# Sixty-four bytes of padding behind each buffer of the split weights

## Chip, cores and metric

The kernel runs on one core of a Trainium2 chip, in one launch. The metric is device time in microseconds of one execution, the median over repeated runs. Times in the text are microseconds (us) unless marked ns.

## What is computed

One layer of a hybrid streaming-encoder block on 256 tokens of width 2,048, in float32:

```python
h = rms_norm(x, mix_norm)
proj = h @ w_in                          # 2048 x 10320, cut into the inputs of both branches
# branch A: causal conv + SiLU, L2-normed q and k, chunked gated delta rule, gated RMSNorm -> o_a
# branch B: latent attention (compressed KV, shared rotary key, block-causal mask)         -> o_b
y = sigmoid(gate_a) * (o_a @ w_branch_a) + sigmoid(gate_b) * (o_b @ w_branch_b)
x = x + y @ w_out
x = x + square(relu(rms_norm(x, mlp_norm) @ w_mlp_up)) @ w_mlp_down      # 2048 -> 8192 -> 2048
x = x + sigmoid(rms_norm(x, ple_norm) @ w_ple_gate) * (p @ w_ple)
```

## The kernel before

**Split operands.** TensorE multiplies in the rounded float32 type `F32R`. To keep float32 accuracy each operand X is written as hi + lo: ScalarE (ACT) copies X into an F32R tile (`act.copy(hi, src)`), and VectorE (DVE) subtracts (`lo = src - hi`). Of the four products the kernel adds three: hi·hi, hi·lo and lo·hi.

**The weight stream.** All large products run in one long loop, `stream`. The weights lie in HBM in the order of use. A step is two 128-row slices of one group of at most 512 columns. `load(i)` brings the step's 512 KB into one of five `raw` tiles through SP's queue; `cut(i)`, three steps ahead of its use, splits it into one of four `whi` and one of four `wlo` tiles; then come the step's matmuls.

**Two kinds of group.** In an ordinary group the activations stand in the array (LDWEIGHTS of 128x128) and the weights move through it, 512 columns at a time; each slice gives six matmuls, all on line L432: for each of two token blocks, activation-hi with `whi`, activation-hi with `wlo`, activation-lo with `whi`. In a turned group (the MLP's up product) the weights stand and the activations `nT` move: per slice four matmuls of 512 columns with `whi` (L425; hi and lo of the 256 tokens side by side) and four of 256 columns with `wlo` (L428). The tiles that hold split activations are `hT`, `cT`, `obT`, `oaT`, `yT`, `nT`, `uT`, `gT` and `pT`; each is 4,096 bytes per partition. The MLP goes up(0), up(1), down(0), up(2), down(1), up(3), down(2), down(3), where up(c) writes `uT` chunk c and down(c) reads it.

**Side work** (norms, transposes, attention, the delta rule) is woven between the steps. Its matmuls are plain float32; the profile records each of them, apart from the transposes, as two passes.

**Pools and places.** Tiles come from pools that lie one behind another in each partition. Behind the weights' pool comes `lpool`, with 23 slots of 4,096 bytes for activations; behind that `tiny`, and then a pool for the mixer's side work whose room the MLP later uses for the pool of the odd `uT` chunks (chunks 0 and 2 are in `lpool`). In `tiny` a 704-byte tile `gap` (`PAD` = 176 floats) is never read. The byte offsets in a partition, as the two built kernels place the tiles:

| tiles | before | after |
|---|---|---|
| `raw`, five | 26,176 + 4,096·n | 26,688 + 4,096·n |
| `whi`, four | 46,656; 50,752; 54,848; 58,944 | 47,168; 51,328; 55,488; 59,648 |
| `wlo`, four | 63,040; 67,136; 71,232; 75,328 | 63,808; 67,968; 72,128; 76,288 |
| `lpool` | 79,424 + 4,096·n | 80,448 + 4,096·n |
| odd `uT` chunks | 187,968 + 4,096·n | 188,992 + 4,096·n |

Before, all but the last row leave 1,600 when divided by 4,096, and the last row leaves 3,648, which is 2,048 more. So the start of every weight tile and the start of every activation tile differ by a multiple of 2,048 bytes; slices of them that meet in one matmul differ by multiples of 512. One pair in the attention is different: `krT` lies at 24,576 (a multiple of 512), `qrT` at 64 bytes past a multiple of 512.

At the start, POOL (GpSimd) clears a tile `spin`, and TensorE runs 14 matmuls on it (L216, output `idle`) while the first weights arrive.

The lines that the prediction speaks of in `stream`:

```python
for j in range(2):
    if g.turned:
        for c in range(4): pe.matmul(ps[c], hi[:, j, cs], g.acts.both(k), ...)           # L425
        for c in range(4): pe.matmul(ps[c][:, :T], lo[:, j, cs], g.acts.both(k)[:, :T])  # L428
    else:
        for tb in range(NT):
            for n_, (part, w) in enumerate(((0, hi), (0, lo), (1, hi))):
                pe.matmul(ps[tb], g.acts.at(k, part, tb), w[:, j, : g.n], ...)           # L432
```

The first operand of `pe.matmul` behind the output stands in the array, the second moves.

Of the kernel before, what the change touches and what calls it, by code (L numbers as in the profile page):

```python
# [9 lines left out]
F32 = mybir.dt.float32  # L10
F32R = mybir.dt.float32r
# [6 lines left out]
P = 128  # L18
# [23 lines left out]
NPIECE = 5  # L42
NSPIN = 14
PAD = 176


def _round12(v):
# [104 lines left out]
def hybrid_block(ctx: ExitStack, tc: tile.TileContext, a, dbg=None):  # L152
    nc = tc.nc
# [6 lines left out]
    wpool = ctx.enter_context(tc.tile_pool(name="wpool", bufs=1))  # L160
# [6 lines left out]
    RAW_BUFS, SPLIT_BUFS, AHEAD, BIG_BUFS = 5, 4, 3, 23  # L167
# [7 lines left out]
    def acc(name):  # L175
        return psA.tile([P, 512], F32, tag="mm", name=name)

    def small(n, name, dt=F32):
        return tiny.tile([P, n], dt, tag=f"t{name}", name=name, bufs=1 if n == 64 else 2)

    gap = tiny.tile([P, PAD], F32, tag="gap", name="gap", bufs=1)
    nc.gpsimd.memset(gap[:, 0:1], 0.0)

# [15 lines left out]
    def load_xT(j):  # L199
        if x_quad[j // 2] is None:  # L200
            x_quad[j // 2] = big(f"xT{j // 2}", shape=(P, 4, T))
        x_pair[j] = x_quad[j // 2][:, 2 * (j % 2) : 2 * (j % 2) + 2, :]
        nc.sync.dma_start(x_pair[j], a["xT"][:, 2 * j : 2 * j + 2, :])
# [24 lines left out]
    def load_rest():  # L228
        tc.keep_in_program_order(nc.sync.dma_start(par, a["par"]))
        yield  # L230
        tc.keep_in_program_order(nc.sync.dma_start(cst, a["cst"]))
        yield
# [29 lines left out]
    def split(hi, lo, src):  # L262

        act.copy(hi, src)
        dve.tensor_tensor(lo, src, hi.bitcast(F32), ALU.subtract)
# [68 lines left out]
    def weave(force=False):  # L334
        clock[0] += 1
        for i in range(len(lanes)):
            n = (clock[1] + i) % len(lanes)
            if (force or clock[0] - lanes[n].last >= lanes[n].gap) and lanes[n].step():
                lanes[n].last = clock[0]
                clock[1] = n + 1  # L340
                return True
        return False

    def until(cond):
        while not cond():
            if not weave(True):
                raise RuntimeError("side work cannot go on")
# [9 lines left out]
    def stream(groups):  # L357
        steps = [(g, k) for g in groups for k in range(0, g.nk, 2)]
        raws, parts = {}, {}

        base, offs = 0, []
        for g, k in steps:
            offs.append(base)
            base += 2 * P * g.n
            PLAN.append((g.srcs, k))

        def load(i):
            n = steps[i][0].n
            t = wpool.tile([P, 2, 512], F32, tag="raw", name=f"raw{i}", bufs=RAW_BUFS)
            src = a["weights"][offs[i] : offs[i] + 2 * P * n].rearrange("(p k n) -> p k n", p=P, k=2)  # L370
            if i == 0:
                for k in range(2):
                    nc.sync.dma_start(t[:, k, :n], src[:, k, :])
            else:
                nc.sync.dma_start(t[:, :, :n], src)
            raws[i] = t

        def cut(i):
            n = steps[i][0].n
            t = raws.pop(i)[:, :, :n]  # L380
            hi = wpool.tile([P, 2, 512], F32R, tag="whi", name=f"whi{i}", bufs=SPLIT_BUFS)
            lo = wpool.tile([P, 2, 512], F32R, tag="wlo", name=f"wlo{i}", bufs=SPLIT_BUFS)
            if i == 0:
                for k in range(2):
                    split(hi[:, k, :n], lo[:, k, :n], t[:, k, :])
            else:
                split(hi[:, :, :n], lo[:, :, :n], t)
            parts[i] = (hi, lo)

        n = len(steps)  # L390
        for i in range(min(RAW_BUFS, n)):
            load(i)
            if i < 3:
                load_xT(i + 1)
        for j in range(4, 8):
            load_xT(j)
        L_CONV.add(load_rest())
        for i in range(min(AHEAD, n)):
            L_TURN.step()
            cut(i)  # L400
        ps, late = None, None
        for i, (g, k0) in enumerate(steps):
            if late and "rx" in done:
                late()
                late = None
            if i + AHEAD < n:
                cut(i + AHEAD)
            if i + RAW_BUFS < n:
                load(i + RAW_BUFS)
            if k0 == 0:  # L410
                if g.before:
                    g.before()
                if g.turned:
                    ps = [g.turned(f"ps{i}_{c}") for c in range(4)]
                else:
                    ps = [acc(f"ps{i}_{tb}")[:, : g.n] for tb in range(NT)]
            hi, lo = parts.pop(i)
            for j in range(2):
                k = k0 + j
                until(lambda: k in g.acts.ready)  # L420
                first, last = k == 0, k == g.nk - 1
                if g.turned:
                    for c in range(4):
                        cs = slice(c * P, (c + 1) * P)
                        pe.matmul(ps[c], hi[:, j, cs], g.acts.both(k), start=first, stop=False)  # L425
                    for c in range(4):
                        cs = slice(c * P, (c + 1) * P)
                        pe.matmul(ps[c][:, :T], lo[:, j, cs], g.acts.both(k)[:, :T], start=False, stop=last)  # L428
# [3 lines that stand above are left out]
                            pe.matmul(  # L432
                                ps[tb], g.acts.at(k, part, tb), w[:, j, : g.n],
                                start=(first and n_ == 0), stop=(last and n_ == 2),
                            )
            if k0 + 2 >= g.nk:
                if "rx" in done:
                    g.evac(ps)
                else:
                    assert late is None  # L440
                    late = bind(g.evac, ps)
            weave()
            weave()
# [864 lines left out]
```

## Time and profile before

| | |
|---|---|
| median of three runs | 1557.18 us (1556.12 to 1558.06) |
| the profiled execution, its own time | 1555.51 us |
| its span, first to last instruction | 1553.6 us |
| TensorE matmuls (PE) busy | 1542.7 us, 99% of the span |
| LDWEIGHTS (PEld) busy | 1309.2 us, 84% |
| DVE, ACT, POOL busy | 979.6, 773.5, 22.8 us |
| granted TensorE clock | 1.000 |

Rows of the profile name source line, engine, operation, output<-inputs and shape. Matmuls are pipelined: a row's "mean ns of one" (some 390 ns for 512 columns) is the time from its start to its modelled end, and overlaps with the next. The pace is the distance from one start to the next, here called the pitch. It is read from the chain that ended last, where a piece "start, length, what xN" is a run of N back-to-back matmuls: the length divided by N is the pitch.

### The profile page before, as it was taken

Reading aid. Unit: us, or ns where it says so; the run is one execution under the profiler, and the core shown is the slowest. Engines: PE = TensorE matmul, PEld = TensorE weight load, DVE = VectorE, ACT = ScalarE, POOL = GpSimd, SP = SyncE. Lnnn points to the kernel's source line nnn. Section 1 sums busy time; section 2 is a strip of 40 time slices with the busy share of each in tenths; the row PEclk is TensorE's granted clock in tenths of the full one; section 3 lists DMA queues with packets and bytes.
Section 4 is the critical chain, followed back from the end, with each engine's and each line's share of the span. In section 5 each row is a group of like instructions: output and inputs, shape, how many; then the busy total and the mean of one; then the engine's idle time right before and its main releaser. Section 6 shows DMA issues by size and latency. Waiting matters only on the chain.

```text
span 1553.6 us, 20822 instructions
## 1 busy us (share of the span) xinstructions
PE 1542.7 (99%) x7760; PEld 1309.2 (84%) x7760; DVE 979.6 (63%) x1715; ACT 773.5 (50%) x1182; POOL 22.8 (1%) x48
## 2 busy tenths in 40 slices
PE   9999999999999999999999999999999999999998
PEld 7998888788888888888888888888888888888888
DVE  6987777965785645755665665556654665555554
ACT  6765776545434544454444443344433443345543
POOL 0000001000100000000000000000000000000000
PEclk9999999999999999999999999999999999999999
DMA  8564434453654555655555555555555555555563
GB/s 305 159 199 165 149 123 167 163 183 136 193 189 157 173 186 195 232 182 187 188 190 190 185 185 197 193 190 187 197 192 189 190 189 191 191 188 187 188 201 116
DMA packets 89415, 286.11 MB, mean 184 GB/s; under 512 B 9632, under 2 KB 22816, under 8 KB 89312
## 3 DMA queue, kind: packets, MB, share of 16 engines
q1 hardware_dynamic: 87168, 281.61, 52.5%
q0 software_dynamic: 1280, 1.84, 0.4%
q10 hardware_dynamic: 864, 1.32, 0.2%
q8 instruction: 61, 1.00, 0.2%
q14 instruction: 42, 0.34, 0.1%
HBM read 282.11 MB, written 2.62 MB: 183 GB/s over the span
## 4 chain that ended last, share of the span: by engine, by line
PE 96%; DVE 2%; ACT 1%; issue 0%; DMA 0%; SPq 0%; DVEq 0%; ACTq 0%
PE ps L432 67%; PE ps L425 15%; PE ps L428 8%; DVE wlo L145 1%; PE tx L985 0%; ACT whi L145 0%; DMA raw<-in_weights 0%; PE sc L703 0%; PE sc L704 0%; DVE strip L145 0%; PE vn L1033 0%; PE kk L895 0%; PE oo L1051 0%; PE kk L894 0%; DVE xsq L145 0%
## 5 line engine op out<-in xcount | busy, mean ns | idle before, releaser
L145 DVE TENSOR_TENSOR wlo<-raw,whi 128x1024 fp32r<-128x1024 f32 (+3 forms) x541 | 644.2, 1192 | 483.1 <-ACT whi L145 480.1
L145 ACT CAST whi<-raw 128x1024 fp32r<-128x1024 f32 (+3 forms) x541 | 555.0, 1027 | 704.5 <-PE ps L432 486.6
L432 PE MATMUL ps<-whi,hT 128*128 128x512 f32 (+2 forms) x1344 | 417.3, 385 | 0.0
L432 PE MATMUL ps<-whi,uT 128*128 128x512 f32 x1024 | 316.0, 389 | 0.0
L432 PEld LDWEIGHTS ps<-whi,hT 128*128 128x128 f32 x1344 | 251.0, 188 | 42.7
L425 PE MATMUL ps<-nT,whi 128*128 128x512 f32 x1024 | 280.5, 395 | 0.0
L432 PE MATMUL ps<-wlo,hT 128*128 128x512 f32 (+2 forms) x672 | 257.2, 383 | 0.3 <-DVE wlo L145 0.3
L432 PEld LDWEIGHTS ps<-whi,uT 128*128 128x128 f32 x1024 | 192.0, 188 | 39.5
L432 PE MATMUL ps<-wlo,uT 128*128 128x512 f32 x512 | 199.5, 390 | 0.0
L425 PEld LDWEIGHTS ps<-nT,whi 128*128 128x128 f32 x1024 | 175.1, 189 | 24.1 <-DVE x L145 0.6
L428 PEld LDWEIGHTS ps<-nT,wlo 128*128 128x128 f32 x1024 | 157.3, 189 | 21.8
L428 PE MATMUL ps<-nT,wlo 128*128 128x256 f32 x1024 | 163.4, 281 | 0.0
L432 PEld LDWEIGHTS ps<-wlo,hT 128*128 128x128 f32 x672 | 126.4, 188 | 21.4 <-DVE wlo L145 0.7
L432 PEld LDWEIGHTS ps<-wlo,uT 128*128 128x128 f32 x512 | 96.1, 188 | 20.0
L432 PE MATMUL ps<-whi,gT 128*128 128x512 f32 (+1 forms) x320 | 82.3, 347 | 0.0
L432 PE MATMUL ps<-whi,yT 128*128 128x512 f32 x256 | 79.7, 391 | 0.0
L432 PEld LDWEIGHTS ps<-whi,gT 128*128 128x128 f32 x320 | 56.1, 189 | 7.5
L432 PEld LDWEIGHTS ps<-whi,yT 128*128 128x128 f32 x256 | 47.8, 188 | 9.6
L432 PE MATMUL ps<-wlo,gT 128*128 128x512 f32 (+1 forms) x160 | 55.5, 347 | 0.0
L432 PE MATMUL ps<-wlo,yT 128*128 128x512 f32 x128 | 50.1, 391 | 0.0
L432 PE MATMUL ps<-whi,oaT 128*128 128x512 f32 x128 | 40.7, 394 | 0.0
L432 PE MATMUL ps<-whi,obT 128*128 128x512 f32 x128 | 39.6, 389 | 0.0
(448 smaller groups left out, 1172.7 us busy)
## 6 DMA issues: line engine op xcount, KB each, us to landing
raw<-in_weights SPq DMA_DIRECT2D x492, 512.0 KB, 3.2
raw<-in_weights SPq DMA_DIRECT2D x24, 384.0 KB, 3.5
raw<-in_weights SPq DMA_DIRECT2D x16, 256.0 KB, 3.1
raw<-in_weights SPq DMA_DIRECT2D x7, 464.0 KB, 7.2
x<-in_x SPq DMA_DIRECT2D x4, 512.0 KB, 7.5
xT<-in_xT SPq DMA_DIRECT2D x7, 256.0 KB, 7.3
blk<-there POOLq DMA_DIRECT2D x8, 128.0 KB, 3.5
cst<-in_cst SPq DMA_DIRECT2D x1, 787.5 KB, 7.5
```

Of the source, the lines that this page charges most:

```text
L145: i = f(*args, **kwargs)
L425: pe.matmul(ps[c], hi[:, j, cs], g.acts.both(k), start=first, stop=False)
L428: pe.matmul(ps[c][:, :T], lo[:, j, cs], g.acts.both(k)[:, :T], start=False, stop=last)
L432: pe.matmul(ps[tb], g.acts.at(k, part, tb), w[:, j, : g.n], start=(first and n_ == 0), stop=(last and n_ == 2),)
```

## The change

A constant `SHIFT` = 16 floats (64 bytes) is added. The `whi` and `wlo` tiles become 1,040 floats long instead of 1,024; the last 16 are not used, and the first 1,024 are viewed as before. A new tile `gap0` of 512 bytes stands ahead of `raw`; its first float is set to zero by POOL. With the eight times 64 bytes of padding it moves everything behind the weights by 1,024 bytes in all.

```diff
+SHIFT = 16
...
+    gap0 = wpool.tile([P, 256 - 8 * SHIFT], F32, tag="gap", name="gap0", bufs=1)
+    nc.gpsimd.memset(gap0[:, 0:1], 0.0)
     gap = tiny.tile([P, PAD], F32, tag="gap", name="gap", bufs=1)
     nc.gpsimd.memset(gap[:, 0:1], 0.0)
...
         def cut(i):
             n = steps[i][0].n
             t = raws.pop(i)[:, :, :n]
-            hi = wpool.tile([P, 2, 512], F32R, tag="whi", name=f"whi{i}", bufs=SPLIT_BUFS)
-            lo = wpool.tile([P, 2, 512], F32R, tag="wlo", name=f"wlo{i}", bufs=SPLIT_BUFS)
+            room = [wpool.tile([P, 1024 + SHIFT], F32R, tag=f"w{s}", name=f"w{s}{i}", bufs=SPLIT_BUFS) for s in ("hi", "lo")]
+            hi, lo = (t[:, :1024].rearrange("p (k n) -> p k n", k=2) for t in room)
```

By the table of places, an `lpool` activation tile now starts, counted modulo 512, 0, 448, 384 and 320 bytes past the four `whi` tiles and 256, 192, 128 and 64 past the four `wlo` tiles. The distances among activation tiles are as before.

The order of instructions on PE, DVE, ACT and SP is the same, row for row. On POOL, at the start of the program, one row is added and two change places (`gap_75` is `gap0`; `spin` is the tile of the 14 first matmuls). Before:

```order
L182 MEMSET gap 128x1
L213 MEMSET ones 128x2
L211 MEMSET spin 128x512
L566 MEMSET krT 64x256
L655 MEMSET qrT_944 64x512
```

and after:

```order
L183 MEMSET gap_75 128x1
L185 MEMSET gap 128x1
L214 MEMSET spin 128x512
L216 MEMSET ones 128x2
L569 MEMSET krT 64x256
```

The clearing of `spin` is the third of these rows in both; `ones` has moved behind it.

## Prediction

> **What bounds the kernel now.** I read the page's head, the waits of PE, the chain and then the groups.
>
> ```profile
> span 1553.6 us, 20822 instructions
> PE 1542.7 (99%) x7760; PEld 1309.2 (84%) x7760; DVE 979.6 (63%) x1715; ACT 773.5 (50%) x1182; POOL 22.8 (1%) x48
> PE 96%; DVE 2%; ACT 1%; issue 0%; DMA 0%; SPq 0%; DVEq 0%; ACTq 0%
> ...
> PE xsum L492 <- DVE xsq L145: 1.7, 1, 1.7
> PE tp_kT L853 <- DVE tmk L145: 1.6, 1, 1.6
> PE idle L216 <- POOL spin L211: 1.4, 1, 1.4
> ...
> PE ps L432 <- DVE wlo L145: 0.3, 1, 0.3
> ```
>
> PE is busy for 1542.7 of 1553.6 us and makes up 96% of the chain. Its longest wait in total is 1.7 us; in the weight stream it waits once, 0.3 us. So the time is the number of matmuls times their pitch, and only what alters the pitch can alter the time by much. The pitch comes from the chain's pieces, length through count:
>
> ```profile
> 65.47 10.41 PE ps L432 x60
> ...
> 917.42 87.07 PE ps L432 x384
> ...
> 1094.45 87.09 PE ps L432 x384
> ...
> 1041.12 0.93 PE ps L425 x4
> 1042.05 0.48 PE ps L428 x4
> ```
>
> The first row is from the 384-column groups: 10.41/60 = 173.5 ns. The next two are down(0) and down(1), 512 columns: 87.07/384 = 226.7 and 87.09/384 = 226.8 ns. 128 columns more cost 53.2 ns, 0.416 ns each; 512 of them make 212.9 ns, and 13.8 ns are left over for every matmul. The last two rows are from up(2), the turned kind: 0.93/4 = 232.5 ns for 512 columns, 0.48/4 = 120 ns for 256.
>
> The two down rows are already an experiment on distance. down(0) reads `uT` chunk 0 from `lpool`, whose tiles leave the same 1,600 as the weights; down(1) reads chunk 1 from the pool that lies 2,048 bytes off. 226.7 against 226.8: that shift moves the pitch by 0.1 ns. What no matmul of the stream shows is a distance that is no multiple of 512 bytes, and these are the distances that the change makes. The nearest rows are the attention's scores, where `knT` and `qnT` are multiples of 512 apart and `krT` lies 448 past the `qrT` slice (modulo 512):
>
> ```profile
> 123.45 0.60 PE L703 MATMUL sc<-knT,qnT 128*128 128x256 f32 x2
> 123.89 0.59 PE L704 MATMUL sc<-krT,qrT 128*128 128x256 f32 x2
> 124.32 0.59 PE L703 MATMUL sc<-knT,qnT 128*128 128x256 f32 x2
> ```
>
> Starts: two passes on `knT` take 0.44 us, two on `krT` 0.43 us, so 216 to 220 ns a pass at either distance. A plain float32 pass of 256 columns takes 216 ns where the F32R matmul of 256 takes 120, so its moving operand is read at about half the rate; the rows are near, not the same.
>
> **The change part by part.**
>
> *The added memset.* POOL's first rows and PE's first:
>
> ```profile
> 0.75 0.10 POOL L182 MEMSET gap<- 128x1 f32 x1 [0.29 <-POOLq L1296]
> 0.78 0.10 POOL L213 MEMSET ones<- 128x2 f32 x1
> 0.82 0.52 POOL L211 MEMSET spin<- 128x512 f32 x1
> ...
> 1.39 5.98 PE L216 MATMUL idle<-spin 128*128 128x512 f32 x14 [1.39 <-POOL spin L211]
> 7.21 0.37 PE L432 MATMUL ps<-whi,hT 128*128 128x464 f32 x1
> ```
>
> PE starts when `spin` is cleared, and the first real matmul follows the spins, so a later `spin` would count in full. But it was third in POOL's row (behind `gap` and `ones`) and is third again (behind `gap0` and `gap`). Cost 0; bounds from the rows' starts, 0.03 to 0.04 us apart: at most 0.04 us either way. `ones` is read first by `xsum`, far later.
>
> *The padding itself* adds no instruction and moves none on PE, DVE, ACT or SP. Four sizes stay: the matmuls' shapes, the splits' shapes, the DMAs and the numbers of buffers. So nothing waits longer for a buffer unless an instruction itself gets slower.
>
> *ACT and DVE* read and write the moved tiles:
>
> ```profile
> L145 DVE TENSOR_TENSOR wlo<-raw,whi 128x1024 fp32r<-128x1024 f32 (+3 forms) x541 | 644.2, 1192 | 483.1 <-ACT whi L145 480.1
> L145 ACT CAST whi<-raw 128x1024 fp32r<-128x1024 f32 (+3 forms) x541 | 555.0, 1027 | 704.5 <-PE ps L432 486.6
> ...
> ACT whi L145 <- PE ps L432: 486.6, 305, 4.1
> ```
>
> A step's two splits take 1027 + 1192 = 2219 ns one behind the other; PE works on a step for 12 x 226.7 = 2720 ns, three steps behind. ACT waits 486.6 us for PE to free `whi`, so the cover is PE itself. DVE would have to grow from 1192 to 2720 ns before it set the pace. Cost 0. If the new distance of `raw` and `whi` made the subtraction cheaper, nothing would come of it either.
>
> *The DMAs* into `raw` land 512 bytes further on:
>
> ```profile
> raw<-in_weights SPq DMA_DIRECT2D x492, 512.0 KB, 3.2
> ```
>
> A slice's landing of 3.2 us stands against five buffers of 2.72 us each. Cost 0.
>
> *TensorE's reading* is what remains. How many matmuls change their distance: by the groups, L432 has 22 forms with 4,944 matmuls, the turned lines 1,024 each.
>
> ```profile
> L432 PE MATMUL ps<-whi,hT 128*128 128x512 f32 x1088 | 348.1, 394 | 0.0
> ...
> L425 PE MATMUL ps<-nT,whi 128*128 128x512 f32 x1024 | 280.5, 395 | 0.0
> ...
> L428 PE MATMUL ps<-nT,wlo 128*128 128x256 f32 x1024 | 163.4, 281 | 0.0
> ...
> L432 PE MATMUL ps<-wlo,pT 128*128 128x512 f32 x16 | 6.3, 394 | 0.0
> ```
>
> One of the eight buffers, the first `whi`, stays at a multiple of 512. Of L432, two thirds (3,296) use `whi`, three quarters of them a moved buffer: 2,472, and with 1,648 on `wlo` 4,120. Of the turned lines 768 and 1,024. Together 5,912 matmuls, so 1 ns of pitch is 5.9 us. Bounds: downwards the pitch could fall to the float32 pass, 216 ns, a gain of 10.7 ns or 63 us. Upwards, what is left over could come twice, +13.8 ns or 82 us. I take 0, since the row nearest to the case, down(1) against down(0), has the same instructions at full rate and shows 0.1 ns for a shift, and the scores show none for 448 bytes.
>
> [...]
>
> Sum: 0 (memset) + 0 (splits) + 0 (DMA) + 0 (pitch). The profiled execution took 1555.51 us, 1.9 over its span and 1.7 below the median of 1557.18; since nothing is added, the forecast is that median, 1557.2 us. The three runs lie within 1 us of it, and 0.2% (3.1 us) is about what a measurement can tell from no change; in pitch that is 3.1/5,912, half a nanosecond.
>
> **The rivals.**
>
> *Slower: reads collide at distances that are not multiples of 512.* Place: L432 with seven of the eight buffers. For it: pitch is not one constant. With weights as the loaded operand it is 232.5 ns (L425) instead of 226.7, so reading conditions can cost 5.8 ns. Against it: L425 meets at multiples of 512 too, so its 5.8 ns don't come from the offset; 8 matmuls in 1.41 us, the 256-column ones every 120 ns, leave the loads less room. Price if the moved matmuls of L432 rise to 232.5: 4,120 x 5.8 ns = 23.9 us, 1581.1 us. It decides from 0.53 ns on.
>
> *Faster: the 13.8 ns that are left over are such a collision, and the old places cause it.* All eight buffers lay alike before, so the trace could not show it otherwise. For it: the float32 pass streams for about as long and leaves only 216 ns from start to start. Against it: that pass is as quick at either distance, and a shift of 2,048 left the 13.8 as they were. Price: all of it 5,912 x 10.7 ns = 63 us, 1494 us; on half the offsets 32 us, 1525.5 us; 3 ns 1539.5 us. It too decides from 0.53 ns on. [...]
>
> *The subtraction becomes the wait.* It needs 2.3 times its 1192 ns; nothing speaks for it. It is in the slower case with 1 in 100.
>
> **How the numbers follow.** No change 50 in 100: two comparisons at other distances show none, but neither is the new distance at the full rate. Slower 30, faster 20: the unknown has both signs, and the shift towards slower is because the stage that reads differently (L425) is the dearer one, while a gain would need a cause that the 2,048-byte shift did not touch. The likeliest case's own range is 1554 to 1561. For 8 in 10, the range goes to 1582, the whole price of the slower rival (beyond it some 8 in 100), and down to 1540, about 3 ns on the moved matmuls (beyond it some 10 in 100).
>
> **What the changed profile would show.** If I am right: pieces of 384 on L432 at 87.0 to 87.2 us in both down stages, the turned four at 0.93 and 0.48 us, DVE and ACT groups at 1192 and 1027 ns give or take 2%, the first matmul at 7.2 us. If a rival is right, the pitch on L432 differs from 226.7 by over half a nanosecond, and it should differ by buffer: every fourth step, whose `whi` is the first, would keep the old pitch in its hi matmuls. What would make me wrong is a dependence on distances below 512 bytes at the full rate, which no row of before can show.

## The result: 0.84% slower

The changed kernel took 1569.88 us (median of 4 runs, 1568.39 to 1571.35), the kernel before 1557.62 us (4 runs, 1556.12 to 1559.21). The ratio is 1.0084, 95% interval 1.0071 to 1.0096: 12.3 us slower. The forecast of no change was wrong; the time lies inside the range of 1540 to 1582, whose upper end was the slower rival's price.

The page's head and the chain by engine, after:

```profile
span 1569.6 us, 20824 instructions
PE 1558.9 (99%) x7760; PEld 1309.1 (83%) x7760; DVE 980.0 (62%) x1715; ACT 771.6 (49%) x1182; POOL 22.9 (1%) x49
PE 95%; DVE 2%; ACT 1%; DMA 1%; issue 0%; SPq 0%; DVEq 0%; ACTq 0%
```

The span grew by 16.0 us and PE's busy time by 16.2 us, at the same number of matmuls. LDWEIGHTS, DVE and ACT are busy for as long as before. So the matmuls themselves run at a slower pitch. (The profiled execution after is the slowest of its four, 1571.35 us; the one before, 1555.51 us, lay 2.1 us below the median of its four. That is why 16.0 stands here against 12.3 between the medians.)

The chain's long pieces show where. L432 is L435 now, L425 and L428 are L428 and L431. A long run in the mixer, down(0), down(1), and the run that starts with down(2), after:

```profile
395.22 74.86 PE ps L435 x324
...
926.90 88.69 PE ps L435 x384
...
1105.05 88.69 PE ps L435 x384
...
1283.20 111.33 PE ps L435 x482
```

and the two of these that were not yet shown of before:

```profile
390.42 73.48 PE ps L432 x324
...
1271.47 109.30 PE ps L432 x482
```

Down stages: 88.69/384 = 231.0 ns against 226.7. The mixer's run: 231.0 against 226.8. Down(2) and on: 231.0 against 226.8. The ordinary groups of 512 columns got 4.2 ns slower in all four of these runs, whichever activations stand in the array. 4,368 of the L432 matmuls have 512 columns, so this makes 18.4 us if the others among them slowed as much. The turned stage went the other way. Up(2) lies between the end of down(0) and the start of down(1): 1105.05 - (926.90 + 88.69) = 89.46 us after, 1094.45 - (917.42 + 87.07) = 89.96 before. Four such stages give 2.0 us back, and 18.4 - 2.0 = 16.4 us agrees with the span's 16.0.

What the prediction had put at nothing is at nothing. The splits, the weight DMAs, and the start, after:

```profile
L146 DVE TENSOR_TENSOR wlo<-raw,whi 128x1024 fp32r<-128x1024 f32 (+3 forms) x541 | 644.4, 1193 | 497.9 <-ACT whi L146 493.2
L146 ACT CAST whi<-raw 128x1024 fp32r<-128x1024 f32 (+3 forms) x541 | 552.8, 1023 | 722.1 <-PE ps L435 501.7
raw<-in_weights SPq DMA_DIRECT2D x492, 512.0 KB, 3.3
0.81 0.53 POOL L214 MEMSET spin<- 128x512 f32 x1
1.40 5.62 PE L219 MATMUL idle<-spin 128*128 128x512 f32 x14 [1.40 <-POOL ones L216]
```

DVE's subtraction is at 1193 ns (1192 before), ACT's copy at 1023 (1027), the landing at 3.3 us (3.2), and PE's first matmul starts at 1.40 us (1.39). The profile puts its wait down to `ones`, but `spin` was cleared at 0.81 + 0.53 = 1.34 us. One sign missed: the first real matmul came at 6.85 us, not 7.2. In the traces of all the kernels here it comes between 6.16 and 7.53 us, while the first spin always starts at 1.39 or 1.40, so the added memset is not the reason.

### The profile page after: what moved, and what is told of

Its sections match the earlier page's. It is cut to its first block, busy times and chain, and to the rows that moved or that the text cites. A ratio compares the mean times of both kernels' runs of the same rounds, so it can differ in the third digit from the quotient of the medians.

```text
span 1569.6 us, 20824 instructions
## 1 busy us (share of the span) xinstructions
PE 1558.9 (99%) x7760; PEld 1309.1 (83%) x7760; DVE 980.0 (62%) x1715; ACT 771.6 (49%) x1182; POOL 22.9 (1%) x49
## 4 chain that ended last, share of the span: by engine, by line
PE 95%; DVE 2%; ACT 1%; DMA 1%; issue 0%; SPq 0%; DVEq 0%; ACTq 0%
PE ps L435 66%; PE ps L428 15%; PE ps L431 8%; DMA raw<-in_weights 1%; DVE wlo L146 1%; ACT whi L146 0%; PE tx L988 0%; PE sc L706 0%; PE sc L707 0%; DVE strip L146 0%; ACT xsq L146 0%; PE vn L1036 0%; PE kk L898 0%; PE oo L1054 0%; PE kk L897 0%
## 5 line engine op out<-in xcount | busy, mean ns | idle before, releaser
L146 DVE TENSOR_TENSOR wlo<-raw,whi 128x1024 fp32r<-128x1024 f32 (+3 forms) x541 | 644.4, 1193 | 497.9 <-ACT whi L146 493.2
L146 ACT CAST whi<-raw 128x1024 fp32r<-128x1024 f32 (+3 forms) x541 | 552.8, 1023 | 722.1 <-PE ps L435 501.7
L435 PE MATMUL ps<-whi,hT 128*128 128x512 f32 (+2 forms) x1344 | 422.5, 389 | 0.0
L435 PE MATMUL ps<-whi,uT 128*128 128x512 f32 x1024 | 320.0, 393 | 0.0
L435 PEld LDWEIGHTS ps<-whi,hT 128*128 128x128 f32 x1344 | 251.9, 189 | 46.8 <-ACT whi L146 0.2
L428 PE MATMUL ps<-nT,whi 128*128 128x512 f32 x1024 | 280.1, 395 | 0.0
L435 PE MATMUL ps<-wlo,hT 128*128 128x512 f32 (+2 forms) x672 | 259.8, 387 | 0.8 <-DVE wlo L146 0.7
L435 PEld LDWEIGHTS ps<-whi,uT 128*128 128x128 f32 x1024 | 192.1, 188 | 43.7
L435 PE MATMUL ps<-wlo,uT 128*128 128x512 f32 x512 | 201.7, 394 | 0.0
L428 PEld LDWEIGHTS ps<-nT,whi 128*128 128x128 f32 x1024 | 174.4, 188 | 23.0 <-DVE x L146 0.6
L431 PEld LDWEIGHTS ps<-nT,wlo 128*128 128x128 f32 x1024 | 156.7, 188 | 22.5
L431 PE MATMUL ps<-nT,wlo 128*128 128x256 f32 x1024 | 161.9, 279 | 0.0
L435 PEld LDWEIGHTS ps<-wlo,hT 128*128 128x128 f32 x672 | 126.8, 189 | 24.2 <-DVE wlo L146 1.4
L435 PEld LDWEIGHTS ps<-wlo,uT 128*128 128x128 f32 x512 | 96.1, 188 | 22.1
L435 PE MATMUL ps<-whi,gT 128*128 128x512 f32 (+1 forms) x320 | 82.7, 348 | 0.0
L435 PE MATMUL ps<-whi,yT 128*128 128x512 f32 x256 | 80.8, 395 | 0.0
L435 PEld LDWEIGHTS ps<-whi,gT 128*128 128x128 f32 x320 | 55.8, 188 | 8.3
L435 PEld LDWEIGHTS ps<-whi,yT 128*128 128x128 f32 x256 | 47.9, 188 | 10.7
L435 PE MATMUL ps<-wlo,gT 128*128 128x512 f32 (+1 forms) x160 | 55.7, 348 | 0.0
L435 PE MATMUL ps<-wlo,yT 128*128 128x512 f32 x128 | 50.6, 395 | 0.0
L435 PE MATMUL ps<-whi,oaT 128*128 128x512 f32 x128 | 41.2, 398 | 0.0
L435 PE MATMUL ps<-whi,obT 128*128 128x512 f32 x128 | 40.0, 392 | 0.0
```

The lines of the kernel that those rows point to most:

```text
L146: i = f(*args, **kwargs)
L435: pe.matmul(ps[tb], g.acts.at(k, part, tb), w[:, j, : g.n], start=(first and n_ == 0), stop=(last and n_ == 2),)
```

## The experiments

Four theories. **R**: the pitch depends on the distance between the slice that moves and the slices that stand or are loaded, with a period of 256 bytes. **A**: it depends on where the moving slice itself starts. **V**: it is buffers that differ from one another that cost time. **S**: the distance between `raw` and the split tiles counts, by way of ACT's and DVE's accesses.

By R, a step's cost should be read from kernels in which all eight buffers have one and the same distance. They are made from the kernel before with spacers, tiles that are not read, put between the weights' tiles: `spacer(name, n)` makes a tile of n floats and sets its first to zero. The code is shown in part; `...` marks what is left out.

### One distance for all: 192 bytes

```diff
+    spacer("gap0", 128)                     # 512 bytes ahead of raw
...
+            if i == 0: spacer("gapA", 48)   # 192 bytes between raw and whi
             hi = wpool.tile([P, 2, 512], F32R, tag="whi", ...)
             lo = wpool.tile([P, 2, 512], F32R, tag="wlo", ...)
+            if i == 0: spacer("gapB", 80)   # 320 bytes behind wlo
```

> All eight split buffers are moved together, by one distance: 192 bytes (modulo 512) past the activation tiles; raw stays level with the activations. Theory R (the distance between the slice that moves through TensorE and the slice that the next LDWEIGHTS reads sets the pitch, with a period of 256 bytes): every L432 matmul of 512 columns gets the pitch that the fourth whi and the last wlo buffer had in the changed kernel, 233.4 ns; a down stage takes 384 x 233.4 ns = 89.6 us, the whole about 1585 us. Rival V (the cost comes from buffers that lie differently from one another): 87.1 us a down stage, 1557 us. Rivals A (where the moving slice itself starts) and S (distance between raw and the split tiles, so ACT's and DVE's accesses) say 89.6 us like R here.

Measured: 1574.4 us (two runs) against 1556.2, ratio 1.0118 (1.0089 to 1.0147). The down stages in the chain:

```profile
927.63 89.60 PE ps L441 x384
1105.88 89.59 PE ps L441 x384
```

89.60/384 = 233.3 ns, as R, A and S have it. Eight buffers that lie alike are slower than eight that differ, so V falls. Up(2) took 1105.88 - (927.63 + 89.60) = 88.65 us, 1.3 less than before. The whole stayed 10.6 us below the 1585 us expected, which had added 6.6 ns on 4,368 matmuls and nothing else. The four turned stages won 5.2 of them. For the rest, the distances between all starts in the two traces show that the ordinary 512-column groups cost 24.8 us more and not 28.8: 104 matmuls that took over 250 ns in the kernel before, beside waits and side work, took 1.4 us less in all, and the other 4,264 grew by 6.1 ns each. The side work's own matmuls took 1.5 us less.

### Weights and activations moved together

```diff
+            if i == 0: spacer("gapA", 48)   # 192 bytes between raw and whi; all behind moves along
             hi = wpool.tile([P, 2, 512], F32R, tag="whi", ...)
```

> Split buffers and activation tiles are moved by the same 192 bytes, raw is not moved. Distance between weights and activations as before, place of both new, distance of raw to the split tiles new. R: 87.1 us a down stage, 1557 us. A and S: 89.6 us a down stage, about 1585 us. V: 87.1 us.

```profile
918.39 87.07 PE ps L438 x384
1095.41 87.09 PE ps L438 x384
```

The same 87.07 and 87.09 us as before the change, to the hundredth; the time 1556.26 us, ratio 1.0 (0.9988 to 1.0011). The moving slices start at the same place modulo 512 as in the last experiment, and the split tiles lie as far from `raw`. A and S fall. Of the four theories only R is left: the distance between weights and activations.

### 64, 128 and 256 bytes

The edit is that of one192 with spacers of 16 and 112, 32 and 96, 64 and 64 floats.

> As one192 with a distance of 64 bytes for all eight split buffers. R: the pitch the changed kernel showed at 64 and 320 bytes, about 229.3 ns on L432, 88.1 us a down stage, turned stages quicker by some 10 ns a slice, the whole about 1565 us. If the pitch at one distance depends on what the neighbouring buffers do, the pure distance gives another value than that mixture.

> As one192 with 128 bytes. R: about 232.3 ns on L432 as at 128 and 384 in the changed kernel, 89.2 us a down stage, the whole about 1582 us less what the turned stages win.

> As one192 with 256 bytes. R with a period of 256: 226.9 ns, 87.1 us a down stage, 1556 us, as before the change. R with a period of 512: another pitch; the 256-byte buffer of step32 showed 232.3 ns, that of the changed kernel 229.5 to 230, which would be 88.2 to 89.2 us a down stage.

The down stages in the chain, first 64 bytes:

```profile
920.23 87.89 PE ps L441 x384
1097.02 87.89 PE ps L441 x384
```

128 bytes:

```profile
929.15 89.24 PE ps L441 x384
1108.34 89.24 PE ps L441 x384
```

and 256 bytes:

```profile
917.56 87.07 PE ps L441 x384
1094.59 87.09 PE ps L441 x384
```

| distance, bytes | down stage, us | pitch, ns | up(2), us | ratio to before (95%) |
|---|---|---|---|---|
| 0 (before) | 87.07 | 226.7 | 89.96 | 1 |
| 64 | 87.89 | 228.9 | 88.90 | 1.0013 (1.0002 to 1.0024) |
| 128 | 89.24 | 232.4 | 89.95 | 1.0135 (1.0106 to 1.0165) |
| 192 | 89.60 | 233.3 | 88.65 | 1.0118 (1.0089 to 1.0147) |
| 256 | 87.07 | 226.7 | 89.96 | 1.0004 (0.9993 to 1.0015) |

At 256 bytes both stages are back to the hundredth of a microsecond, and at 64, 128 and 192 they are not: in steps of 64 bytes, the period is 256. Each of 0, 64, 128 and 192 belongs to two of the changed kernel's eight buffers. The mean of the four down stages is (87.07 + 87.89 + 89.24 + 89.60)/4 = 88.45 us; the changed kernel took 88.69. So 1.38 of the 1.62 us that the padding costs a down stage are the mean of four distances, three of them worse than the one it replaced; the rest, 0.24 us, comes with the mixing.

The trace of the changed kernel shows how it comes. The built kernel gives the buffers to the steps in the order first, fourth, third, second, and a step's `whi` and `wlo` lie at the same distance modulo 256; so the steps run at 0, 192, 128, 64 bytes and again. From the starts in down(0), the pitch per step is 228.8, 233.3, 232.5 and 229.3 ns on average, near the pure values except at 0. There the first five matmuls behind the 64-byte step take 231, 236, 228, 232 and 231 ns, and the last seven 226.7 each. Eight such steps lose 8 x 24.6 ns = 0.20 us, most of the 0.24: a matmul seems to hand part of its delay on to the next.

For 64 bytes the expectation of 1565 us was too high (1559.45); the turned stages won 1.06 us each, 4.2 us in all. For 128 bytes they won nothing, and the time, 1576.8 us (two runs), is still 5 us below the 1582 expected.

### Without loads and splits

The kernel with 192 bytes for all (one192), with this in its loop, shortened:

```diff
             if i + AHEAD < n:
-                cut(i + AHEAD)
+                if i + AHEAD < 12: cut(i + AHEAD); kept[i + AHEAD] = parts[i + AHEAD]
+                else: parts[i + AHEAD] = kept[8 + (i + AHEAD) % 4]
-            if i + RAW_BUFS < n:
+            if i + RAW_BUFS < 12:
```

> one192, with loads and splits only for the first 12 steps of the weight stream: all later steps multiply with the split buffers of steps 8 to 11 again. What is left out: the loads and splits of the other steps, so its result is not the layer. No weight DMA and nearly no ACT or DVE work runs beside the matmuls. R as a matter of TensorE's own two reads: 233.3 ns on L432 at 512 columns all the same, 89.6 us a down stage. If the distance acts by way of ACT's or DVE's or the DMA's accesses: back to 226.9 ns, 87.1 us.

Busy times, the casts that are left, and the down stages:

```profile
PE 1561.6 (99%) x7760; PEld 1307.1 (83%) x7760; DVE 374.1 (24%) x1187; ACT 250.3 (16%) x652; POOL 23.1 (1%) x51
...
L145 ACT CAST whi<-raw 128x928 fp32r<-128x928 f32 (+2 forms) x13 | 11.9, 923 | 5.1 <-DMA raw<-in_weights 3.8 <-DVE hT L145 1.3
...
926.21 89.59 PE ps L445 x384
1104.41 89.59 PE ps L445 x384
```

Against one192, DVE's busy time fell from 979.8 to 374.1 us, ACT's from 772.4 to 250.3, and only the first 12 steps' weight DMAs are left. In down(0) itself, over 89.4 us, DVE is busy for 9.5 us (48.0 in one192), ACT for 2.4 (35.3), and the DMA engines for 1% of the time (59%). The down stages stay at 89.59 us. So the splits and the weight loads have no part in the cost that these two runs show, and what is left, by exclusion, is TensorE's own reading of its two operands. (One run; the same kernel at distance 0 was not run, so the comparison is with one192.)

### Finer steps

The change with `SHIFT = 8`, once as it is and once with all views 16 bytes further on (`t[:, 4:1028]`).

> The change with 32 bytes of padding instead of 64: distances 256 to 480 in steps of 32 (modulo 512), from the first whi to the last wlo. R with a period of 256: the buffers at 256, 320, 384 and 448 repeat the pitches that 0, 64, 128 and 192 had in the changed kernel (L432, 512 columns: about 227, 229, 232, 233 ns), the odd multiples of 32 lie between their neighbours; a down stage 88.3 to 88.9 us, the whole 1566 to 1571 us. If distances below 64 bytes matter by themselves, a buffer at an odd multiple of 32 leaves that band. A and V: no such repetition; V about 1570 us.

> As step32, and all eight views start 16 bytes later in their tiles: distances 272 to 496 in steps of 32. R, smooth: each buffer lies between its neighbours of step32, a down stage within 0.5 us of step32's. If the 13.8 ns left over per matmul are a collision that some fine distance avoids, a buffer here or in step32 shows under 222 ns on L432 at 512 columns; R does not require it, and the faster rival of the prediction does.

The down stages in the chain, 32-byte steps from 256 on:

```profile
927.66 89.16 PE ps L435 x384
1106.56 89.16 PE ps L435 x384
```

and from 272 on:

```profile
922.79 88.31 PE ps L435 x384
1100.99 88.31 PE ps L435 x384
```

1574.4 us (two runs) and 1566.0 us (three; ratios 1.0118, 1.0089 to 1.0147, and 1.0068, 1.0045 to 1.0091). The first is 0.3 us a stage over what was expected, the second 0.85 us below the first where 0.5 was allowed. Read by buffer, from the distances between starts of all 512-column L432 matmuls in the trace, no buffer came below 228.2 ns on average. So the faster rival found no distance there. But the reading by buffer does not hold what was hoped of it: the `whi` at 256 bytes shows 232.3 ns here, and the eight buffers of one256 show 227.1. With 32 bytes of padding a step's `whi` and `wlo` lie 128 bytes apart modulo 256, so every step mixes two distances, and a matmul's pitch depends on its neighbours' distances too. These two runs say nothing sure on single distances below 64 bytes.

### Each kind of group at its own distance

Turned stages do better at 192 bytes, ordinary ones at 0 or 256. Buffers 256 bytes longer allow both. To make room, `PAD` went from 176 to 48 and the tile `kr` from two buffers to one. The diff is against the changed kernel and leaves these two out.

```diff
-SHIFT = 16
+SHIFT = 64
...
-    gap0 = wpool.tile([P, 256 - 8 * SHIFT], F32, tag="gap", name="gap0", bufs=1)
-    nc.gpsimd.memset(gap0[:, 0:1], 0.0)
...
-            hi, lo = (t[:, :1024].rearrange("p (k n) -> p k n", k=2) for t in room)
+            at = (48, 48) if steps[i][0].turned else (0, 0)
+            hi, lo = (r[:, o : o + 1024].rearrange("p (k n) -> p k n", k=2) for r, o in zip(room, at))
```

> Each split buffer is 256 bytes longer, so that all eight lie level with the activations modulo 256; in the turned groups alone the split weights are put 192 bytes further on in their buffers. R: L432 as before (87.1 us a down stage), the turned stages as in one192, where their 8 matmuls of a slice took 1384 ns against 1403 before: 256 slices x 19.4 ns = 5.0 us less, 1552 us, ratio 0.997. V (buffers that differ) and A (absolute places, here eight of them): slower than before.

```profile
917.40 87.06 PE ps L434 x384
1093.20 87.06 PE ps L434 x384
```

1552.44 us against 1556.63: ratio 0.9971 (0.9960 to 0.9983), 0.3% faster than the kernel before. Down stages as before; up(2) takes 1093.20 - (917.40 + 87.06) = 88.74 us, 1.22 less, four times 4.9 us. The places of the eight buffers differ here, and by V or A the kernel would have been slower than before.

Three more with other offsets in the turned groups, `at = (0, 16)`, `(56, 56)` and `(40, 40)`:

> As turned192, with the turned groups' hi weights at 0 and their lo weights at 64 bytes. It tells which loaded slice counts. If the pitch of a matmul goes by the slice that is loaded meanwhile for the next one: the fourth hi matmul of a slice (it runs while the first lo slice is loaded) goes from 228.4 to about 236 ns, the fourth lo matmul (the next hi slice is loaded) stays at 118.3. If it goes by the slice that stands in the array already: the fourth hi matmul stays at 228.4, the fourth lo matmul falls to 113.6.

> As turned192 with 224 bytes. R, if the pitch changes smoothly with the distance: between 192 (1384 ns a slice) and 256 (1402 ns), so 2 to 3 us less than before, about 1554.5 us. If it is better than 192, the fine distance has more to give.

> As turned192 with 160 bytes. R, smooth: between 128 (1404 ns a slice) and 192 (1384 ns), so 2 to 3 us less than before, about 1554.5 us.

Down(0) and down(1) of the three, in this order:

```profile
918.81 87.07 PE ps L434 x384
1095.63 87.07 PE ps L434 x384
```

```profile
918.51 87.06 PE ps L434 x384
1095.30 87.06 PE ps L434 x384
```

```profile
921.35 87.07 PE ps L434 x384
1098.99 87.07 PE ps L434 x384
```

Up(2) takes 89.75, 89.73 and 90.57 us; the times are 1556.49 us (one run), 1555.11 (ratio 0.9990, 0.9981 to 1.0000) and 1559.43 (1.0017, 1.0008 to 1.0026). 224 bytes won 1.5 us where 2 to 3 were expected. 160 bytes is worse than 128 (89.95 us, one128) and 192 on either side of it: between the multiples of 64 the pitch is not smooth, and that expectation fails. As the three share turned192's `PAD` and `kr` and do not gain its 4.2 us, the gain comes from the offset. The first of the three was to tell whether the loaded or the standing slice counts, and does not. By starts, in the second slice of each step, the fourth hi matmul took 229 ns and the fourth lo matmul 119.9, so neither 236 with 118.3 nor 228.4 with 113.6; and the second and third hi matmuls, whose own distances did not change, went from 234.5 and 232.0 to 235.7 and 228.4. A delay handed on, as in the mixture above, would do this. Which of the two slices counts stays open.

## Why the prediction was wrong, point by point

- *What bounds the kernel*: right. Only the pitch could move the time, and it did.
- *Memset, splits, DMAs*: right, each at nothing, by the rows above.
- *TensorE's reading, taken at 0*: this step failed. It measured 4.2 ns on 4,368 matmuls, and half a microsecond the other way in each turned stage. The pitch depends on the distance modulo 256 between weights and activations (226.7 to 233.3 ns in the kernels with one distance for all), and the padding gave six of the eight buffers a new one (the first `wlo`, counted as moved, lies at 256). The bounds of -10.7 and +13.8 ns held it, the choice within them was wrong. That the time fell into the range shows only that the range allowed for a mechanism that the forecast had put at nothing. The rows that the choice leaned on could not carry it. Down(1) against down(0) shifts by 2,048 bytes, eight whole periods of 256, so that no dependence with that period can show. The scores' 448 bytes are no multiple of 256, but they are float32 passes at about half the rate (216 ns for 256 columns, where the F32R matmul takes 120); what one kind shows need not hold for the other, and why the scores show nothing, no run here tested. The text said that these rows were near and not the same, and then let them decide. At 192 bytes the cost stays with loads and splits left out, 6.6 ns a matmul (233.3 in still192 against 226.7 before); how the two operands come to affect each other, the runs do not show.
- *The slower rival*: the right case, at 30 in 100. Its price of 5.8 ns on 4,120 matmuls (23.9 us) was 18.4 us on L432. The distance does cost that much (6.6 ns at 192 bytes), though the turned stage from which it reasoned has its 232.5 ns at distance 0, and why is open; the 2.0 us which the turned stages won were in nobody's sum.
- *The faster rival*: the 13.8 ns left over were not removed by any distance tried. No ordinary stage went below 226.7 ns a matmul; only the turned groups had a better place than the old one.
- *Showing it by buffer*: in part. The first `whi` was to keep 226.7 ns and showed 229.4 on average over the kernel; in down(0) the last seven matmuls of its steps do keep 226.7, and the first five carry the delay of the step before.

## What to carry to other kernels

A control has to be checked for whether it could have shown the effect at all: a shift by 2,048 bytes tests nothing that repeats every 256. In a kernel bound by TensorE, as this one is (PE busy for 99% of the span), the distance of its two operands modulo 256 is worth a scan with one distance per kernel and not eight in one: here it moved the ordinary groups' pitch between 226.7 and 233.3 ns. Each kind of product can have its own best value: of the distances tried here, 0 where the weights move (226.7 ns) and 192 bytes where they stand (88.74 us for up(2) against 89.96), together worth 0.3%.

## What the runs showed of the hardware that was not expected

The pitch of back-to-back F32R matmuls with 512 moving columns, each with an LDWEIGHTS of its own, depends on the distance of their operands in a partition: 226.7, 228.9, 232.4 and 233.3 ns at 0, 64, 128 and 192 bytes, and 226.7 again at 256. With DVE and ACT busy for 9.5 and 2.4 of 89.4 us and the DMA engines for 1%, it is 233.3 ns at 192 as well. Moving both operands together by 192 bytes changes nothing (226.7 ns). Of the 226.7 ns, the prediction's estimate gives 212.9 to the 512 columns (0.416 ns each, from 173.5 ns at 384) and leaves 13.8; the best distance tried leaves all 13.8 in ordinary groups, and what they are stays open.
